# Strassen's identity for a feed-forward matrix of the first layer, token-major, with 16 transposes

## The chip, the cores and the metric

The kernel runs on one core of a Trainium2 chip. The metric is the device time of one execution in microseconds (us), the median of several runs. The core's engines work side by side and wait for each other through semaphores: PE (TensorE) multiplies matrices, DVE (VectorE) and ACT (ScalarE) do elementwise work, POOL (GpSimd) does a little of it, and SP, POOL and ACT issue DMA transfers. Results of PE land in PSUM, which has eight banks of 128 x 512 numbers here; all else lies in SBUF.

## The reference

A trunk of two layers over 256 tokens with 1024 features. Each layer is a token mixer (a gated linear recurrence in the first, causal attention with a bias by relative position in the second) followed by a feed-forward part, each with an RMS norm in front and a residual add behind; a last norm closes it.

```python
def swiglu(h, w13, w2):
    g, u = jnp.split(h @ w13, 2, axis=-1)
    return ((jax.nn.silu(g) * u) @ w2).astype(h.dtype)

for layer in range(2):
    h = h + mixer(rms_norm(h, norm_mix[layer]))
    h = h + swiglu(rms_norm(h, norm_ffn[layer]), ffn_w13[layer], ffn_w2[layer])
return rms_norm(h, final_norm)
```

w13 is 1024 x 5632 and w2 is 2816 x 1024, so the hidden width is 22 tiles of 128. Everything is float32.

## The kernel before

**Number format.** PE multiplies in a rounded format (`fp32r`). To keep float32's precision each operand is split into a high part (ACT, L448 for weights: `whi`) and the rest (DVE, L450: `wlo`), and each product is three matmuls: high x high, high x low, low x high. A product with a 128 x 128 weight as the stationary operand and 256 tokens as the moving one is `mm_w`; a product with 128 tokens of an activation as the stationary operand and 512 weight columns as the moving one, token-major, is `mm_x`.

**Weights.** All weights lie in DRAM in the order of their use (`weight_plan`), in units of 1024 columns. A unit is loaded by SP into one of the `raw` buffers (six, taken in turn), split into one of `NSUB` = 6 pairs `whi`, `wlo`, and then used. `make_subs` keeps the units coming some way ahead. `keep["from"]` holds the pairs back from reuse while a later part still reads them.

**Order of the work.** A planner (`Order`) writes out, while the program is built, the order of instructions on each engine. PE's main stream is fixed by the code; it advances the planner's clock `now` and a count of tiles. Every other operation has an estimated cost, what it depends on, and a due time in tiles; each engine's queue takes, among the operations that are ready, the one due first. An operation is ready 130 ns (`LAT`) after what it depends on. `od.need` makes the main stream wait in the plan. On the chip each engine then runs its list in that order and waits where semaphores tell it.

**First layer's feed-forward (`swiglu(0, ...)`).** For each hidden tile j: gate and up (48 matmuls, PSUM group A), then on ACT and DVE Sigmoid and three products, the split into `hh`, `hl`, and, four tiles later, the row j of w2 times this tile (`down0`, 24 matmuls, four banks of group B, feature-major: eight feature tiles of 128 x 256 tokens). The last two rows are taken bank by bank, and each finished bank goes to `residual`, which scales it by the norm's `row`, adds it to the residual `hT`, and makes the next layer's split input `x2`.

**Second layer's feed-forward.** Here w2 is taken by Strassen's identity already. Two hidden tiles make one step: a 2 x 2 block of tokens (two halves of 128) by hidden tiles, times a 2 x 2 block of hidden tiles by output columns (two halves of 512). Seven products m1 to m7 stand for eight. `combine` makes the sums of activations, `quad_sums` those of weights: one difference (`wdiff`), one sum on DVE (L480), one sum by an accumulating DMA on POOL's queue (L488; for the last step on DVE, L484). `early` takes m1, m2, m5 and `late` takes m4, m3, m6, m7; each m accumulates in a PSUM bank of its own over nine steps. The last four hidden tiles are not in steps: their rows go straight, by `mm_x`, into the banks of m6, m3, m7 and m2, which turns these into the four output quadrants. `fold` adds the other shares (m1, m5, m4, and m2 and m3 for a quadrant not their own) on DVE to `ht`, the residual turned to token-major by 16 transposes (L1334). The last step's folds, but that of m3, wait for the last weight split. `od.need` on `read` keeps PE from adding to m2 and m3 before their fold has read them.

Of the kernel before, what the change touches and what calls it, by code (L numbers as in the profile page):

```python
# [8 lines left out]
FT = mybir.dt.float32  # L9
# [6 lines left out]
P = 128  # L16
# [20 lines left out]
def quad(k):  # L37

    return [("ffn_w2", 1, k + a, 512 * b, 512) for a, b in ((0, 1), (1, 0), (1, 1), (0, 0))]


def weight_plan():
# [28 lines left out]
    def ffn(layer):  # L71
        for k in range(KT - 2):
            for j in range(4):
                plan.append(("ffn_w13", layer, k, P * j, P))
                plan.append(("ffn_w13", layer, k, DFF + P * j, P))
        for j in range(4):
            for half in range(2):
                column("ffn_w13", layer, half * DFF + P * j, (KT - 2, KT - 1))

        for j in range(4, FTN):  # L80
            column("ffn_w13", layer, P * j)
            column("ffn_w13", layer, DFF + P * j)
            if layer == 0:
                rows("ffn_w2", layer, j - 4)
            elif (j % 2 and 4 < j < FTN - 1) or j == FTN - 2:
                plan.extend(quad(j - 5 + j // (FTN - 2)))
        if layer == 0:
            for k in range(FTN - 4, FTN - 2):
                rows("ffn_w2", layer, k)
            last_rows("ffn_w2", layer, FTN)  # L90
        else:
            for k in range(FTN - 4, FTN):
                for nh in range(2):
                    plan.append(("ffn_w2", layer, k, 512 * nh, 512))
# [32 lines left out]
class Ring:  # L127
# [3 lines left out]
    def new(self, held=False):  # L131
        b = Buf(self)
        b.held = held
        return b

# [5 lines left out]
class Order:  # L141
# [38 lines left out]
    def free_at(self, ring):  # L180

        if len(ring.past) < ring.bufs:
            return 0.0
        b = ring.past[-ring.bufs]
# [24 lines left out]
    def emit(self, o, t):  # L209
# [11 lines left out]
        for b in o.alloc:  # L221
            b.tile = b.ring.make()
            b.ring.past.append(b)
# [87 lines left out]
def hybrid_trunk(ctx: ExitStack, tc: tile.TileContext, wts, xT, par, gfin, tab, onehot, masks, out):  # L311
# [29 lines left out]
    def lay_out():  # L341
# [13 lines left out]
        sb.tile([P, 16], FT, name="gape")  # L355
        for part in "hl":
            ring(f"e{part}0", [P, S], 1, FR).make()
        sb.tile([P, 48], FT, name="gapf")

# [32 lines left out]
    lay_out()  # L392
    segs, c0 = [], 0
# [5 lines left out]
    for i, e in enumerate(plan):  # L399
        if plan[i:i + 4] == quad(e[2]):  # L400
            quads[[a for a, _ in segs].index(c)] = e[2]
# [27 lines left out]
    def make_subs(upto):  # L429

        while ws["made"] < min(upto, len(subs)):
# [25 lines left out]
            ws["V"] = ov  # L457
            ws["made"] += 1
# [7 lines left out]
    diffs, sums = {}, {}  # L466
# [613 lines left out]
    for k in range(KT):  # L1080
# [14 lines left out]
    od.op("A", ca(P), lambda: A.activation(heads(tbh.tile), many, AF.Copy), reads=[tb], alloc=[tbh], due=80)  # L1095
    od.op("V", cv(P), lambda: V.tensor_tensor(heads(tbl.tile), many, heads(tbh.tile.bitcast(FT)), op=OP.subtract),
          reads=[tb, tbh], alloc=[tbl], due=80)
    od.op("A", ca(NOH), lambda: A.activation(ohr.tile, oh.tile, AF.Copy), reads=[oh], alloc=[ohr], due=80)
    for eb, c0, n in zip(ebs, (0, 384), (384, NOH - 384)):
        def biases(eb=eb, c0=c0, n=n):  # L1100
            mm(eb[:, :n], tbh.tile, ohr[:, c0:c0 + n], start=True)
            mm(eb[:, :n], tbl.tile, ohr[:, c0:c0 + n], stop=True)
        od.op("T", 500, biases, reads=[tbh, tbl, ohr], alloc=[eb], due=80)
        al = dict(writes=[e]) if c0 else dict(alloc=[e])
        od.op("A", ca(n), lambda eb=eb, c0=c0, n=n: A.activation(e[:, c0:c0 + n], eb[:, :n], AF.Copy), reads=[eb],
              due=80, **al)
# [49 lines left out]
    def swiglu(layer, x, stats, gu, down):  # L1156

        hs = {}

        def hidden(j, b):  # L1160
            gs = new("sgq", [P, S], 3)
            sg = new("u", [P, S], 3)
            due = 6
            od.op("V", cv(S), lambda: V.tensor_tensor(gs.tile, b[:, :S], stats.row.tile, op=OP.mult),
                  reads=[b, stats.row], alloc=[gs], due=due)
            od.op("A", ca(S), lambda: A.activation(sg.tile, gs.tile, AF.Sigmoid), reads=[gs], alloc=[sg], due=due)
            od.op("V", cv(S), lambda: V.tensor_tensor(gs.tile, gs.tile, sg.tile, op=OP.mult), reads=[sg], writes=[gs], due=due)
            od.op("V", cv(S), lambda: V.tensor_tensor(sg.tile, b[:, S:], gs.tile, op=OP.mult), reads=[b, gs], writes=[sg],
                  due=due)
            x = X("e", 0, 1) if (layer, j) in ((0, 0), (0, 11)) else X("h", j % 7)  # L1170
            hi, lo = x.h, x.l
            od.op("A", ca(S), lambda: A.activation(hi.tile, sg.tile, AF.Copy), reads=[sg], alloc=[hi], due=due + 6)
            od.op("V", cv(S), lambda: V.tensor_tensor(lo.tile, sg.tile, hi.tile.bitcast(FT), op=OP.subtract),
                  reads=[sg, hi], alloc=[lo], due=due + 6)
            hs[j] = x

        first_four(layer, [main_bank(gu) for _ in range(4)], x, hidden)
        for j in range(4, FTN):
            b = main_bank(gu)
            gate_up(layer, j, b, x)  # L1180
            hidden(j, b)
            b.held = False
            od.written(stats.row)
            down(j - 4, hs)
        for k in range(KT):
            x[k].free()
        down(FTN - 4, hs, last=True)
# [3 lines left out]
    acc = {}  # L1191

    def down0(k, hs, last=False):
        if not acc:
            acc[0] = [main_bank("B") for _ in range(4)]
        for kk in range(k, FTN if last else k + 1):
            out_rows("ffn_w2", 0, kk, hs, acc[0], FTN, lambda i: residual(i, acc[0][i], x2, 1, st2, st1.row, 4 * i))

    od.written(sto.row)
    swiglu(0, x1, st1, "A", down0)  # L1200


    st2.finish("B", 40)
# [3 lines left out]
    vv.ring.past.append(vv)  # L1207

# [96 lines left out]

    def more_raws():

        old, turn = rings["raw"], [0]

        def make():  # L1310
            turn[0] += 1
            return bt.tile[:, 2 * D:3 * D] if turn[0] % (RAW + 1) == 1 else old.make()
        rings["raw"] = Ring(make, RAW + 1)
        rings["raw"].past = [Buf(None)] + old.past[-RAW:]
        inside("wsum", D, SUB, 1)
# [7 lines left out]
    more_raws()  # L1323
# [85 lines left out]
    alias("uu", "mov", [P, 512])  # L1409
    alias("gu", "sqacc", [P, 512])  # L1410
    alias("wdiff", "yt", [P, 512])
    inside("xdiff", 0, P, 2, e)
    QUADS = (FTN - 4) // 2
    hs, ops, pair = {}, {}, {}

    def hidden1(j, b, copied):
        s = new("sgq", [P, S], 3)
        due = 2
        if copied:
            g = new("gu", [P, 512], 2)  # L1420
            od.op("A", ca(512), lambda b=b: A.activation(g.tile, b[:, :], AF.Copy), reads=[b], alloc=[g], due=0)  # L1421
            b = g
        od.op("V", cv(S), lambda: V.tensor_tensor(s.tile, b[:, :S], st3.row.tile, op=OP.mult),  # L1423
              reads=[b, st3.row], alloc=[s], due=due)
        od.op("A", ca(S), lambda: A.activation(s.tile, s.tile, AF.Silu), reads=[s], writes=[s], due=due)
        up = (b, lambda: b[:, S:])
        if j < 2 * QUADS:
            if j % 2 == 0:
                pair[j // 2] = new("uu", [P, 512], 2)
            u = pair[j // 2]  # L1430
            c = slice(j % 2 * S, j % 2 * S + S)
            od.op("V", cv(S), lambda: V.tensor_tensor(u[:, c], up[1](), s.tile, op=OP.mult), reads=[up[0], s], due=due,
                  **(dict(writes=[u]) if j % 2 else dict(alloc=[u])))
            if j % 2:
                combine(j // 2, u)
            return
        u = new("u", [P, S], 3)
        od.op("V", cv(S), lambda: V.tensor_tensor(u.tile, up[1](), s.tile, op=OP.mult), reads=[up[0], s], alloc=[u],  # L1438
              due=due)
        hs[j] = X("h", (4 * QUADS + j - 2 * QUADS) % 7)  # L1440
        split(hs[j], u, lambda: u.tile, S, due + 4)

    def split(x, b, src, n, due):
        hi, lo = x.h, x.l
        r = (lambda t: t) if n != "z" else lambda t: t.rearrange("p (z t) -> p z t", z=2)
        n = S if n == "z" else n
        od.op("A", ca(n), lambda: A.activation(r(hi[:, :n]), src(), AF.Copy), reads=[b], alloc=[hi], due=due)
        od.op("V", cv(n), lambda: V.tensor_tensor(r(lo[:, :n]), src(), r(hi[:, :n].bitcast(FT)), op=OP.subtract),
              reads=[b, hi], alloc=[lo], due=due)

    def combine(p, u):

        a, b, d = new("sgq", [P, S], 3), new("u", [P, S], 3), new("xdiff", [P, P], 2)
        due = 6
        ops[p] = {t: X("h", (4 * p + n) % 7) for n, t in enumerate("dacb")}
        od.op("V", cv(P), lambda: V.tensor_tensor(d.tile, u[:, :P], u[:, 384:], op=OP.subtract), reads=[u], alloc=[d],
              due=due)
        split(ops[p]["d"], d, lambda: d.tile, P, due)
        od.op("V", cv(S), lambda: V.tensor_tensor(a.tile, u[:, :S], u[:, S:], op=OP.subtract), reads=[u], alloc=[a],
              due=due)  # L1460
        split(ops[p]["a"], a, lambda: a.tile, S, due)
# [150 lines left out]
```

## Time and profile before

| | |
|---|---|
| Median of 3 runs | 609.55 us (609.29 to 609.84) |
| Profiled execution, its own time | 608.73 us |
| Span from its first to its last instruction | 607.0 us |
| Granted PE clock, mean | 0.997 |
| Busy: PE, DVE, ACT, POOL | 598.1, 476.2, 387.7, 53.4 us |
| First layer's feed-forward, tiles in their steady order | about 175 to 316 us |
| Second layer's feed-forward | about 433 to 601 us |

In the profile's rows a number such as x48 counts instructions, the first two numbers are start and duration in us (in lists by time), `psA<-whi,hh` means that the instruction wrote a tile of PSUM group A from the tiles `whi` and `hh`, and what stands in square brackets is idle time before it and what ended it. A row of busy time by stretch gives its bounds, its length, and for PE, PE's weight loads, DVE, ACT and POOL busy us and instructions, then the granted clock, the DMA engines' busy share and GB/s. Matmul ends are modelled; their starts show PE's pace.

### The profile page before, as it was taken

What the parts mean: (1) busy time and instruction counts of PE and PEld (TensorE: products, weight loads), DVE (VectorE), ACT (ScalarE), POOL (GpSimd) and SP (SyncE); (2) the same over time, 40 slices, a digit from 0 to 9 for tenths busy, and PEclk for the clock granted to TensorE, in tenths of its full rate; (3) what the DMA queues carried; (4) which work ended last, traced back from release to release, by engine and by line L of the source; (5) the groups of instructions that cost most, each with busy time, mean ns of one, the idle gap of its engine ahead of it and who ended that gap; (6) DMA issues with size and microseconds to landing.
All of it is one profiled execution on the core that took longest, in us unless ns stands there. A gap on an engine that the chain in (4) does not pass through costs nothing.

```text
span 607.0 us, 12428 instructions
## 1 busy us (share of the span) xinstructions
PE 598.1 (99%) x4783; PEld 579.3 (95%) x4783; DVE 476.2 (78%) x869; ACT 387.7 (64%) x761; POOL 53.4 (9%) x101
## 2 busy tenths in 40 slices
PE   9999999999999999999999999999999999999995
PEld 7899999999999999999998899999999999999985
DVE  6899988869665766666669578876889798889896
ACT  6798998947634554444447566664777576666763
POOL 0043131100321000000000100000000000000003
PEclk9999999999999999999999999999999999999998
DMA  8956543554799766656563564446475677678721
GB/s 290 348 174 201 182 141 118 164 172 134 212 188 258 271 189 195 197 188 205 182 202 113 202 215 167 144 150 229 158 200 169 225 234 236 203 255 237 205 70 69
DMA packets 34406, 116.68 MB, mean 192 GB/s; under 512 B 4683, under 2 KB 6219, under 8 KB 34348
## 3 DMA queue, kind: packets, MB, share of 16 engines
q1 hardware_dynamic: 31484, 109.05, 54.0%
q0 software_dynamic: 1904, 6.10, 6.3%
q10 hardware_dynamic: 960, 0.76, 0.5%
q8 instruction: 37, 0.61, 0.4%
q14 instruction: 21, 0.17, 0.1%
HBM read 114.51 MB, written 1.38 MB: 191 GB/s over the span
## 4 chain that ended last, share of the span: by engine, by line
PE 93%; DVE 5%; issue 1%; POOL 1%; ACT 0%; DVEq 0%; POOLq 0%; ACTq 0%
PE psB L532 51%; PE psA L532 41%; DVE wlo L450 2%; DVE xl L656 0%; POOL ny L706 0%; PE psB L1276 0%; DVE yt L722 0%; DVE hT L724 0%; DVE sqacc L674 0%; PE psA L1334 0%; DVE ii L1486 0%; ACT whi L448 0%; DVE u L1438 0%; PE psA L711 0%; DVE sgq L1423 0%
## 5 line engine op out<-in xcount | busy, mean ns | idle before, releaser
L450 DVE TENSOR_TENSOR wlo<-raw,whi 128x1024 fp32r<-128x1024 f32 (+1 forms) x200 | 238.8, 1204 | 79.2 <-ACT whi L448 78.5
L448 ACT ACTIVATE whi<-raw 128x1024 fp32r<-128x1024 f32 (+1 forms) x199 | 205.5, 1045 | 118.5 <-PE psA L532 48.5
L532 PE MATMUL psB<-xh,whi 128*128 128x256 f32 x608 | 171.4, 285 | 0.0
L532 PE MATMUL psB<-xh,wlo 128*128 128x256 f32 x608 | 166.5, 277 | 0.0
L532 PE MATMUL psB<-xl,whi 128*128 128x256 f32 x608 | 162.0, 277 | 0.0
L532 PE MATMUL psA<-xh,whi 128*128 128x256 f32 x544 | 151.1, 281 | 0.0
L532 PE MATMUL psA<-xh,wlo 128*128 128x256 f32 x544 | 148.7, 277 | 0.0
L532 PE MATMUL psA<-xl,whi 128*128 128x256 f32 x544 | 143.6, 277 | 0.0
L532 PEld LDWEIGHTS psB<-xh,wlo 128*128 128x128 f32 x608 | 114.5, 188 | 0.7
L532 PEld LDWEIGHTS psB<-xh,whi 128*128 128x128 f32 x608 | 114.4, 188 | 0.7
L532 PEld LDWEIGHTS psB<-xl,whi 128*128 128x128 f32 x608 | 111.4, 188 | 0.0
L532 PEld LDWEIGHTS psA<-xh,whi 128*128 128x128 f32 x544 | 102.3, 188 | 0.2
L532 PEld LDWEIGHTS psA<-xh,wlo 128*128 128x128 f32 x544 | 102.3, 188 | 0.0
L532 PEld LDWEIGHTS psA<-xl,whi 128*128 128x128 f32 x544 | 99.2, 188 | 0.0
L532 PE MATMUL psB<-hl,whi 128*128 128x256 f32 x160 | 44.2, 276 | 0.0
L532 PE MATMUL psB<-hh,whi 128*128 128x256 f32 x160 | 44.2, 276 | 0.0
L532 PE MATMUL psB<-hh,wlo 128*128 128x256 f32 x160 | 44.2, 276 | 0.0
L706 POOL TENSOR_TENSOR ny<-nv,mhalf 128x2 f32<-128x2 f32 x5 | 5.6, 1111 | 304.0 <-DVE nv L703 281.6
L532 PEld LDWEIGHTS psB<-hh,whi 128*128 128x128 f32 x160 | 30.0, 188 | 0.0
L532 PEld LDWEIGHTS psB<-hh,wlo 128*128 128x128 f32 x160 | 30.0, 188 | 0.0
L532 PEld LDWEIGHTS psB<-hl,whi 128*128 128x128 f32 x160 | 30.0, 188 | 0.0
L1421 ACT ACTIVATE gu<-psB 128x512 f32<-128x512 f32 x18 | 10.8, 598 | 26.3 <-PE psB L532 26.3
(239 smaller groups left out, 936.8 us busy)
## 6 DMA issues: line engine op xcount, KB each, us to landing
raw<-in_w_dram SPq DMA_DIRECT2D x193, 512.0 KB, 4.3
bt<-in_w_dram SPq DMA_DIRECT2D x9, 512.0 KB, 4.9
raw<-in_w_dram POOLq DMA_DIRECT2D x7, 512.0 KB, 5.4
hT<-in_x_dram SPq DMA_DIRECT2D x8, 128.0 KB, 5.0
raw<-in_w_dram SPq DMA_DIRECT2D x4, 256.0 KB, 4.6
bt<-scr POOLq DMA_DIRECT2D x16, 64.0 KB, 9.7
bt<-scr POOLq DMA_DIRECT2D x2, 256.0 KB, 11.6
bt<-in_final_dram ACTq DMA_DIRECT2D x1, 512.0 KB, 5.2
```

Of the source, the lines that this page charges most:

```text
L448: oa = od.op("A", ca(n), lambda h=h, r=src, o=o, n=n: A.activation(h[:, :n], r[:, o:o + n], AF.Copy), reads=[src], alloc=[h], due=due)
L450: ov = od.op("V", cv(n), lambda h=h, lo=lo, r=src, o=o, n=n: V.tensor_tensor(lo[:, :n], r[:, o:o + n], h[:, :n].bitcast(FT), op=OP.subtrac ...
L532: T.matmul(o, a, b, start=start, stop=stop, skip_group_check=True)
L706: od.op("G", 500, lambda: G.tensor_tensor(y.tile, v.tile, mhalf, op=OP.pow), reads=[v], alloc=[y], due=due)
L1421: od.op("A", ca(512), lambda b=b: A.activation(g.tile, b[:, :], AF.Copy), reads=[b], alloc=[g], due=0)
```

## The change

The second layer's code becomes a class `Strassen` that both layers use. In the first layer:

- All rows of w2 but the last four go in nine Strassen steps, with `gu` copies, Silu, `combine`, `quad_sums` and POOL's accumulating DMAs as in the second layer. Group A holds m1, m5, m4 and one bank for gate and up; group B holds m6, m3, m7, m2.
- The output quadrants are token-major, and there is no `ht` to add to: token half 0 goes to the first half of `vv` and half 1 to two `yq` buffers (in the place of `yt`). The first fold of each quadrant fills its buffer (a TENSOR_SCALAR), later ones add.
- The final four rows are taken in the order m6, m3, m7, m2. After each pair of quadrants, PE turns them by eight transposes into two banks of group B (`turned`), and `residual` adds these to `hT` with no further scaling.
- Raw buffers are handed out by the first that is free (`Slots`), with the second half of `vv` as a seventh during the first layer's steps, and two places in `bt` during the second layer's in the place of one.
- The position bias's operations get earlier due times, and its DMAs later and staggered ones.

```diff
+class Slots:
+    def first(self, order):
+        best = None
+        for s in self.slots:
+            t = None if not s[2] else 0.0 if s[1] is None else order.done(s[1])
+            if t is not None and (best is None or t < best[0]):
+                best = t, s
+        return best
...
+        def fold(self, i, *to):
+            m, col = self.m[i], self.stats.col
+            for tt, nh, plus, due in to:
+                c = col if plus else self.minus
+                q, at = self.quadrants[tt, nh]
+                first = (tt, nh) not in self.filled
+                self.filled.add((tt, nh))
+                def add(c=c, at=at, tt=tt, first=first):
+                    if first:
+                        V.tensor_scalar(at(), m[:, :], c[:, tt:tt + 1], None, op0=OP.mult)
+                    else:
+                        V.scalar_tensor_tensor(at(), m[:, :], c[:, tt:tt + 1], at(), op0=OP.mult, op1=OP.add)
+                kw = dict(alloc=[q]) if first and q.ring is not None else dict(writes=[q]) if first else {}
+                o = od.op("V", cv(512), add, reads=[m, c] if first else [m, q, c], due=due, **kw)
+                if i != 3:
+                    o.deps.append(self.behind)
...
+            if p == QUADS - 1:
+                self.behind = splits[w.i + 8]
+                self.fold(1, (0, 1, True, 35), (1, 0, True, 46))
+                self.fold(5, (0, 1, True, 35), (0, 0, False, 44))
+                self.fold(2, (1, 0, False, 45))
...
+                self.fold(4, (0, 1, True, 15), (1, 1, True, 25))
+                self.fold(3, (1, 0, True, 0))
...
+    f = Strassen(0, x1, st1, "A", {"A": (1, 5, 4), "B": (6, 3, 7, 2)}, quadrants)
+    w = {(k, nh): piece("ffn_w2", 0, k, 512 * nh, 512) for nh in range(2) for k in f.ks}
+    extra[2] = False
+    def turned(i, nh):
+        b = bank("B")
+        def turn():
+            for j in range(2):
+                for tt in range(2):
+                    c = 256 * (i % 2) + P * j
+                    T.transpose(b[:, S * j + P * tt:S * j + P * tt + P], quadrants[tt, nh][1]()[:, c:c + P], ident)
+        od.op("T", 450, turn, reads=[quadrants[tt, nh][0] for tt in range(2)], alloc=[b], due=0, early=700.0)
+        residual(i, b, x2, 1, st2, None, 2)
+    for nh, tt in ((0, 1), (0, 0), (1, 0), (1, 1)):
+        b = f.final[nh, tt]
+        f.wait_fold(nh, tt)
+        for k in f.ks:
+            mm_x(b[:, :], f.hs[k], w[k, nh], tt, stop=(k == FTN - 1))
+        wrote(b)
+        b.held = False
+        q, at = quadrants[tt, nh]
+        od.op("V", cv(512), lambda b=b, at=at, tt=tt: V.scalar_tensor_tensor(
+            at(), b[:, :], st1.col[:, tt:tt + 1], at(), op0=OP.mult, op1=OP.add), reads=[b, q, st1.col], writes=[q],
+            due=0).deps.extend(f.folds[tt, nh])
+        if (nh, tt) in ((0, 0), (1, 1)):
+            turned(2 * nh, nh)
+            turned(2 * nh + 1, nh)
...
-    od.op("G", 1000, lambda: G.dma_start(scr, e.tile), ...)           # bias operations ahead of this: due=80
+    od.op("G", 1000, lambda: G.dma_start(scr, e.tile), ...)           # bias operations ahead of this: due=40
-              nbytes=262144, due=90)
+              nbytes=262144, due=100 + r // 4)
-                  reads=[scr_b], writes=[bt], nbytes=65536, due=90)
+                  reads=[scr_b], writes=[bt], nbytes=65536, due=136 + r + 4 * j)
```

More of the change, by code (lines that the diff above doesn't have):

```diff
@@ L82, in ffn @@
             column("ffn_w13", layer, DFF + P * j)
[L83 to L94, printed above, removed]
+            if (j % 2 and 4 < j < FTN - 1) or j == FTN - 2:
+                plan.extend(quad(layer, j - 5 + j // (FTN - 2)))
+        last = [(k, nh) for k in range(FTN - 4, FTN) for nh in range(2)]
+        for k, nh in last if layer else sorted(last, key=lambda p: p[::-1]):
+            plan.append(("ffn_w2", layer, k, 512 * nh, 512))
     token_major("hgrn_w_in", 2 * D)
@@ L134, in new, with __init__, take @@
         return b
+class Slots:
+    def __init__(self, tiles):
+        self.slots = [[t, None, True] for t in tiles]
+    def new(self, held=False):
+        b = Buf(self)
+        b.held = held
+        return b
+    def first(self, order):
[5 more added lines that the diff above has]
+        return best
+    def take(self, b, order):
+        s = self.first(order)[1]
+        b.tile, s[1] = s[0], b
 class Op:
@@ L1154, in gate_up @@
         wrote(b)
[L1156 to L1162, printed above, removed]
-            due = 6
[L1164 to L1168, printed above, removed]
-                  due=due)
[L1170 to L1187, printed above, removed]
@@ L1207, in hybrid_trunk @@
     vv.ring.past.append(vv)
+    extra = [vv.tile[:, 1, :], None, True]
+    rings["raw"].slots.append(extra)
+    part0 = [Buf(None) for _ in range(2)]
+    quadrants = {(0, nh): (part0[nh], lambda nh=nh: vv[:, 0, 512 * nh:512 * nh + 512]) for nh in range(2)}
+    for nh in range(2):
+        yq = new("yq", [P, 512], 2)
+        quadrants[1, nh] = yq, lambda yq=yq: yq.tile
+    f = Strassen(0, x1, st1, "A", {"A": (1, 5, 4), "B": (6, 3, 7, 2)}, quadrants)
[24 more added lines that the diff above has]
+            turned(2 * nh + 1, nh)
+    for k in f.ks:
+        f.hs[k].free()
+    keep["from"] = None
+    free_subs(ws["sub"])
+    for i in (1, 4, 5):
+        f.m[i].held = False
+    od.need(lambda: 0.0 if extra[1] is None else od.done(extra[1]))
+    st2.finish("B", 40)
     vsplit = {}
@@ L1322, in hybrid_trunk @@
     st3.finish("A", 14)
-    more_raws()
+    for i in (1, 2):
+        rings["raw"].slots.append([bt.tile[:, D * i:D * i + D], None, True])
     gf = Buf(None)
@@ L1443, in split @@
[L1443 to L1461, printed above, removed]
-        split(ops[p]["c"], u, lambda: cut(u, 0, (384, 2), (1, P)), "z", due + 1)
-        od.op("V", cv(S), lambda: V.tensor_tensor(
-            b.tile.rearrange("p (z t) -> p z t", z=2), u[:, P:384].rearrange("p (z t) -> p z t", z=2),
-            cut(u, 0, (384, 2), (1, P)), op=OP.subtract), reads=[u], alloc=[b], due=due + 1)
-        split(ops[p]["b"], b, lambda: b.tile, S, due + 1)
@@ L1523, in hybrid_trunk @@
-    first_four(1, [main_bank("B") for _ in range(4)], x3, lambda j, b: hidden1(j, b, False))
-    for j in range(4, FTN):
-        if j < 7:
-            b = one = main_bank("B")
-        else:
-            last = b
-            od.need(lambda: None if any(o.end is None for o in last.readers) else max(o.end for o in last.readers))
-            b = Buf(None)
-            b.tile = one.tile
-        gate_up(1, j, b, x3)
-        b.held = j == 6
-        hidden1(j, b, True)
-        if j == 4:
-            od.op("A", ca(D), lambda: A.activation(gf.tile, gf.tile, AF.Copy, scale=2 * float(D) ** 0.5), reads=[bt],
-                  writes=[gf], due=30)
-        if j > 4:
-            (early if j % 2 and j < FTN - 1 else late)((j - 5) // 2)
-        if j == FTN - 2:
-            early(QUADS - 1)
```

277 lines of the change are left out of this document (157 added, 120 removed).

## The prediction

> **What bounds the kernel now.** I read the engine totals first, then the chain of work that ended last, in order of time, then the busy time of two stretches: the plain feed-forward of the first layer (168 to 307 us) and the Strassen feed-forward of the second (457 to 575 us).
>
> ```profile
> PE 598.1 (99%) x4783; PEld 579.3 (95%) x4783; DVE 476.2 (78%) x869; ACT 387.7 (64%) x761; POOL 53.4 (9%) x101
> ...
> PE 93%; DVE 5%; issue 1%; POOL 1%; ACT 0%; DVEq 0%; POOLq 0%; ACTq 0%
> ...
> 168.00:307.00 139.00, 139.00 (x1226) 139.00 (x1226) 89.11 (x122) 65.04 (x86) 5.26 (x10) 1.00 0.71 209
> 457.00:575.00 118.00, 118.00 (x881) 111.62 (x880) 104.41 (x156) 78.77 (x121) 6.12 (x7) 1.00 0.73 223
> ...
> 294.22 5.44 PE psA L532 x48
> 299.66 2.72 PE psB L532 x24
> ...
> 457.87 2.06 PE psA L532 x9
> 459.93 6.15 PE psB L532 x51
> 466.08 0.69 PE psA L532 x3
> 466.77 6.84 PE psB L532 x54
> 473.61 2.06 PE psA L532 x9
> ...
> 427.71 1.75 PE psA L1334 x16
> ```
>
> The reader is to see that PE is never idle in either stretch (139.00 of 139.00, 118.00 of 118.00). So PE work taken out is gained in full, and a PE wait put in is lost in full. The two layers differ in their cover: VectorE (third busy figure) has 89.11/139 = 64% in the first layer, 104.41/118 = 88% in the second. The chain rows give prices: a moving operand of 256 columns costs 5.44/48 = 0.113 us, one of 512 columns 2.06/9 = 0.229 us, a transpose 1.75/16 = 0.109 us. A hidden tile of the first layer costs 5.44 + 2.72 = 8.16 us (gate and up, then its row of w2); two of them, 16.32 us. In the second layer two hidden tiles with one Strassen step run from 457.87 to 473.61, 15.74 us.
>
> **The change part by part.** *The nine Strassen steps.* Each replaces 48 matmuls of 256 columns by 21 of 512: 5.44 - 21 x 0.229 = 0.63 us by count. By whole periods it is 16.32 - 15.74 = 0.58 us. I take the periods, since they hold the changes between banks too: 9 x 0.58 = 5.2 us off PE (5.7 by count).
>
> *The last four rows of w2*, token-major: 48 x 0.229 = 11.0 us in place of 4 x 2.72 = 10.9: +0.1.
>
> *The 16 transposes* go through PE between matmuls, +1.75 us. With nothing else, PE work falls by 5.2 - 0.1 - 1.75 = 3.35 us.
>
> *VectorE and ScalarE in the steady part.* The first layer takes over the second's load: four weight splits and two sums per step, the gate copies to SBUF, Silu for Sigmoid and two products. In the second layer that fits under PE without one idle moment, so I cost it at nothing; without that cover a split is late by its length. VectorE's eighth of time to spare is thin. Silu may ask ScalarE for one table load more, which lies in its free third.
>
> *Queues.* SP's loads become 7 for 6 in two hidden tiles, POOL gets eight accumulating DMAs, and the 18 DMAs of the position bias now share POOL's queue with them. The bias operations come earlier. Raw buffers by the first that is free change nothing while PE never waits for a load. These cost nothing as long as weight units stand ready; that cover is priced as a rival.
>
> *The end of the layer* is where I see a new wait. I take it from the end of the second layer, with the last product group there from 585.69, after which the final products begin at 588.43.
>
> ```profile
> 585.69 0.39 PE L532 MATMUL psB<-whi,hh 128*128 128x512 f32 x1
> 588.43 0.28 PE L532 MATMUL psB<-whi,hh 128*128 128x256 f32 x1
> ...
> 586.38 1.06 ACT L448 ACTIVATE whi<-raw 128x1024 fp32r<-128x1024 f32 x1
> ...
> 586.99 0.42 DVE L1423 TENSOR_TENSOR sgq<-gu,rrow 128x256 f32<-128x256 f32 x1
> 587.32 0.74 DVE L1486 SCALAR_TENSOR_TENSOR ii<-psA,ny,ii 128x512 f32<-128x512 f32 x1
> 587.98 1.22 DVE L450 TENSOR_TENSOR wlo<-raw,whi 128x1024 fp32r<-128x1024 f32 x1
> 589.12 0.42 DVE L1438 TENSOR_TENSOR u<-gu,sgq 128x256 f32<-128x256 f32 x1
> 589.45 0.74 DVE L1486 SCALAR_TENSOR_TENSOR ii<-psA,ny,ii 128x512 f32<-128x512 f32 x1
> 590.12 0.41 DVE L1448 TENSOR_TENSOR hl<-u,hh 128x256 fp32r<-128x256 f32 x1
> 590.45 0.74 DVE L1486 SCALAR_TENSOR_TENSOR ii<-psA,ny,ii 128x512 f32<-128x512 f32 x1
> 591.23 0.75 DVE L1486 SCALAR_TENSOR_TENSOR ii<-psB,ny,ii 128x512 f32<-128x512 f32 x1
> 591.89 0.74 DVE L1486 SCALAR_TENSOR_TENSOR ii<-psA,fm,ii 128x512 f32<-128x512 f32 x1
> ...
> 594.92 0.74 DVE L1486 SCALAR_TENSOR_TENSOR ii<-psA,ny,ii 128x512 f32<-128x512 f32 x1
> ...
> L1404 DVE TENSOR_SCALAR raw<-raw,fz x2: 380/384/389, 602.7 to 603.0; 128x320 f32<-128x320 f32 x2
> ```
>
> PE may not add the last four rows into bank m3 before the fold of m3 has read it. In the second layer that fold (587.32) waits for nothing else, since it adds into `ht`, which is filled already. In the first layer its target is a `yq` buffer that a fold of m1 must first fill, and this one must wait for the layer's last weight split (`behind`), with a due time of 46, after five other folds with 35, 44 and 45. The second layer's rows show that order: the m1 fold to this place is the last, at 594.92, over 5 us behind the first. So I rebuild VectorE's queue with these durations. The last split starts when its high part is made, 586.38 + 1.06 = 587.44, and takes 1.14 to the next start: 588.6. Then u of the last hidden tile (0.33): 588.95. Then six folds and one split of u, 6 x 0.66 + 0.34 = 4.3: 593.25. Four of the folds are fill operations of another form; by the TENSOR_SCALAR row, 0.384 us for 320 columns, 512 would be about 0.6, which takes 0.2 to 0.3 off. The planner calls an operation ready 130 ns after what it depends on, so behind the m1 fold the next weight unit (the value projection's first, 1.14) can slip in before m3's fold (0.74). m3 is read at 594.0 without and 595.1 with it. PE, after 12 products for m6, stands ready at 588.43 + 12 x 0.229 = 591.2. It waits 2.8 to 3.9 us; I take 3.4, the slip with cheap fills. The bounds are 0, if the folds come early enough, and 4.5, if VectorE is half a split later than here. Nothing else is queued for PE there: the transposes need the same quadrants.
>
> *After it.* Five of the six pairs of split weights are held until the final products end. The value projection's second unit is split after that, 1.06 + 1.22 = 2.3 us, under 12 products of its first unit (2.75 us) and eight transposes (0.9 us): nothing, or up to 1 us if VectorE has a residual in front. The residual loses its four scaling products. The first four feature tiles are turned two final quadrants before they are needed.
>
> ```profile
> 336.01 0.43 PE L711 MATMUL psB<-ident,ny 128*128 128x128 f32 x2 [0.62 <-POOL ny L706]
> ```
>
> PE waits here for POOL's power (0.62 us). I leave it in; it could go, 0.6 less.
>
> **The sum** against the profiled execution's span: 607.0 - 5.2 + 0.1 + 1.75 + 3.4 = 607.05. That execution took 608.73 and the median of the runs is 609.55, so 2.5 us lie around the span: 609.6.
>
> **The rivals.** *Faster: the folds are in time.* If m3's fold is done by 591.2 on that clock, the whole 3.35 us stay: 606.2. It decides at 2.8 to 3.9 us of VectorE time, the folds that would have to go elsewhere. For it: of the six only the one fold of m1 to that quadrant must be ahead of m3's. Against: the due times.
>
> *Slower: weight units late while the bias DMAs run.*
>
> ```profile
> 164.00:172.00 8.00, 8.00 (x72) 8.00 (x71) 7.40 (x15) 4.70 (x9) 3.21 (x7) 1.00 0.91 118
> 180.00:188.00 8.00, 8.00 (x73) 8.00 (x72) 3.40 (x6) 2.44 (x3) 3.08 (x6) 1.00 1.03 243
> 196.00:204.00 8.00, 8.00 (x73) 8.00 (x72) 7.19 (x11) 4.75 (x7) 0.00 (x0) 1.00 0.91 323
> ...
> ACT whi L448 <- DMA raw<-in_w_dram: 12.5, 7, 3.5
> ...
> 193.79 1.23 DVE L450 TENSOR_TENSOR wlo<-raw,whi 128x1024 fp32r<-128x1024 f32 x1 [1.31 <-ACT whi L448]
> 201.53 0.28 PE L532 MATMUL psB<-hh,wlo 128*128 128x256 f32 x1
> ...
> 457.32 1.22 DVE L450 TENSOR_TENSOR wlo<-raw,whi 128x1024 fp32r<-128x1024 f32 x1
> 465.46 0.39 PE L532 MATMUL psB<-wlo,hh 128*128 128x512 f32 x1
> ...
> 482.15 1.22 DVE L450 TENSOR_TENSOR wlo<-bt,whi 128x1024 fp32r<-128x1024 f32 x1
> 486.58 0.28 PE L532 MATMUL psB<-xh,wlo 128*128 128x256 f32 x1
> ```
>
> The DMA engines are full from 164 to 204 us (0.91 to 1.03 of their time), and ScalarE waits 12.5 us for raw weights between 156 and 200. PE feels nothing, since the split that ends at 195.0 is first used at 201.5: 6.5 us in hand. In the second layer a split that ends at 483.4 is used at 486.6: 3.2 us in hand. The first Strassen steps fall into the full stretch and ask for a sixth more loads. If the 12.5 us of lateness meet 3 us in hand, PE loses about 2 us there (0 to 4): 611.6 with the wait above. Against it: the bias DMAs start earlier, and the second layer's first step has 6.9 us in hand (a split ends at 458.5, its use is at 465.5).
>
> *Slower: the new gap halves PE's clock.*
>
> ```profile
> 600.50:603.70 3.20, 0.04 (x1) 0.00 (x0) 2.42 (x9) 1.65 (x6) 0.84 (x1) 1.00 0.36 145
> 603.80:607.00 3.20, 0.00 (x0) 0.00 (x0) 0.00 (x0) 0.00 (x0) 0.00 (x0) 0.50 0.47 164
> ```
>
> The granted clock goes from 1.00 to 0.50 some 3.2 us after PE's last work (600.54). A wait of 3.2 us or more could meet that; if PE then ran at half clock for as long again, it would lose 1.6 us: 611.2. [...]
>
> **How the numbers follow.** Wait of 2.8 to 3.9 us and nothing more, 40%: 609.6, between 608.4 and 610.7. Folds in time, or half so, 30%: 606.2 to 608.4. Late weights, 22%: 610.7 to 613. Half clock, 8%. Range 606.0 to 612.6, which leaves out the ends of both. A difference of 0.2% (1.2 us) is about what a measurement here can tell. Faster 0.32 (folds in time, and a little of the main case with the POOL wait gone), same 0.38, slower 0.30.
>
> **What would show it.** Right: 16.32 us of the first layer become 15.7 in the chain, with no PE gap in the steps after the first; near the layer's end PE idles once, about 3 us, and its releaser is a VectorE fold; that fold stands behind six others and perhaps a weight split. Wrong: no gap there (then 606), gaps near 190 to 210 us with ScalarE waiting for raw weights, or a granted clock of 0.5 behind the gap.

## The result, and the profile after

The changed kernel takes 614.59 us (median of 4 runs, 613.18 to 616.04) against 609.58 us for the kernel before on the same chip: a ratio of 1.0082, interval 1.0059 to 1.0106. It is slower by 5.0 us, where 609.6 was forecast and the range ended at 612.6. Its profiled execution took 616.04 us, with a span of 614.3 us and a mean granted clock of 0.992.

The engine totals, and the chain of work that ended last by engine, of the changed kernel:

```profile
PE 599.2 (98%) x4508; PEld 568.4 (93%) x4508; DVE 514.7 (84%) x938; ACT 414.3 (67%) x816; POOL 61.7 (10%) x109
...
PE 91%; DVE 4%; DMA 2%; issue 1%; ACT 1%; POOL 1%; DVEq 0%; POOLq 0%; ACTq 0%
```

PE runs 275 matmuls fewer, and is still busy as long as before (599.2 us for 598.1). DMA and ACT, which had next to nothing of the chain, now have 3% of it.

**The steps themselves came out as forecast.** The chain in order of time (start, length, what):

```profile
218.29 2.06 PE psB L556 x9
220.34 6.15 PE psA L556 x51
226.50 0.69 PE psB L556 x3
227.19 6.84 PE psA L556 x54
234.03 2.06 PE psB L556 x9
```

Two hidden tiles take 234.03 - 218.29 = 15.74 us, with no idle time in between.

**Early wait.** The same view, in the second and third step:

```profile
184.03 1.15 DVE wsum L504
...
185.46 11.54 DMA raw<-in_w_dram
...
197.09 1.06 ACT whi L471
...
198.83 1.22 DVE wlo L473
...
201.80 1.15 DVE wlo L473
```

and PE's own rows, with its idle time in brackets:

```profile
200.11 0.50 PE L556 MATMUL psA<-wlo,hh 128*128 128x512 f32 x1 [1.27 <-DVE wlo L473]
...
202.99 0.51 PE L556 MATMUL psB<-wlo,hh 128*128 128x512 f32 x1 [1.22 <-DVE wlo L473]
```

VectorE must have read the plain weights for its own sum (`wsum`) before POOL may add to them by its accumulating DMA; that DMA is issued at 185.46 and has landed 11.54 us later; its split comes too late, and PE waits twice. These two start 1.66 and 1.61 us after the matmul before them, where the pace is 0.229: 2.8 us lost. Four of the dozen matmuls behind the first also start late, by 0.1 us each, against the same ones in e5 below, which has no such wait. The early wait costs 3.2 us in all.

**Wait at the layer's end.** VectorE's queue, and PE's first final product into m3 (start, length, line, operation):

```profile
308.19 1.23 DVE L473 TENSOR_TENSOR wlo<-ii,whi 128x1024 fp32r<-128x1024 f32 x1 [0.53 <-ACT whi L471]
309.33 0.42 DVE L1253 TENSOR_TENSOR u<-gu,sgq 128x256 f32<-128x256 f32 x1
309.67 0.75 DVE L1311 TENSOR_SCALAR ii<-psA,ny 128x512 f32<-128x512 f32 x1
310.33 0.74 DVE L1311 TENSOR_SCALAR ii<-psA,fm 128x512 f32<-128x512 f32 x1
310.99 0.41 DVE L1263 TENSOR_TENSOR hl<-u,hh 128x256 fp32r<-128x256 f32 x1
311.32 1.53 DVE L1313 SCALAR_TENSOR_TENSOR ii<-psA,ny,ii 128x512 f32<-128x512 f32 x2
312.77 1.40 DVE L1311 TENSOR_SCALAR yq<-psA,ny 128x512 f32<-128x512 f32 x2
314.08 1.22 DVE L473 TENSOR_TENSOR wlo<-raw,whi 128x1024 fp32r<-128x1024 f32 x1
315.21 0.75 DVE L1313 SCALAR_TENSOR_TENSOR yq<-psB,ny,yq 128x512 f32<-128x512 f32 x1
```

```profile
316.01 0.79 PE L556 MATMUL psB<-whi,hh 128*128 128x512 f32 x1 [3.94 <-DVE yq L1313]
```

This is the predicted queue: last split, six folds, the next weight unit slipped in at 314.08, then m3's fold. PE's matmul before it started at 311.67, so the two starts are 4.34 us apart, 4.1 more than the pace.

**Half clock.** Busy time by stretch (bounds, length; PE, PE's weight loads, DVE, ACT, POOL; then the granted clock):

```profile
311.60:314.70 3.10, 0.47 (x3) 0.04 (x1) 3.06 (x5) 0.00 (x0) 0.00 (x0) 1.00 0.02 7
314.70:316.00 1.30, 0.00 (x0) 0.00 (x0) 1.26 (x3) 0.00 (x0) 0.00 (x0) 0.50 0.00 0
316.00:321.50 5.50, 5.49 (x13) 4.33 (x14) 1.50 (x2) 0.00 (x0) 0.00 (x0) 0.50 0.31 95
321.50:324.60 3.10, 3.10 (x20) 2.62 (x19) 1.46 (x3) 0.00 (x0) 0.00 (x0) 1.00 0.03 5
```

The clock falls to 0.50 while PE waits, and stays there for 5.5 us of work: eleven matmuls start 0.427 us apart in place of 0.229, and with the ones at either end PE loses 2.6 us.

**The balance.** I compare one stretch, from the same matmul of the first layer's token mixer to the same matmul of the second layer's: two rows of before, then two of the changed kernel.

```profile
131.38 0.28 PE L532 MATMUL psB<-xh,wlo 128*128 128x256 f32 x1
...
358.32 0.28 PE L532 MATMUL psA<-xh,whi 128*128 128x256 f32 x1
```

```profile
132.63 0.28 PE L556 MATMUL psB<-xh,wlo 128*128 128x256 f32 x1
...
344.47 0.43 PE L735 MATMUL psB<-ident,ny 128*128 128x128 f32 x2 [0.73 <-POOL ny L730]
...
365.86 0.28 PE L556 MATMUL psA<-xh,whi 128*128 128x256 f32 x1
```

It grew from 226.94 to 233.23 us, by 6.3: +3.2 early wait, +4.1 wait at the end, +2.6 half clock, +0.1 POOL's power (0.73 for 0.62 us of idle time). That leaves -3.7 for PE's work, where the forecast had -3.35. The spans differ by 7.3; the other 1.0 is the start, which came 1.25 us later, less 0.2 behind the stretch. The change does not touch the start: over the profiles of this case but e9's, that first matmul starts between 130.8 and 132.6 us. From 24 to 48 us PE's matmuls of 256 columns start 0.118 us apart here and 0.113 to 0.114 in the kernel before; e10, an edit of the kernel before, has 0.118 as well, and no row shows why. Below, "the stretch" is the one between the two matmuls, and its length is free of that chance. This profile is the slowest of the four executions, 1.45 us above their median.

### The profile page after: what moved, and what is told of

Its sections match the earlier page's. It is cut to its first block, busy times and chain, and to the rows that moved or that the text cites. A ratio compares the mean times of both kernels' runs of the same rounds, so it can differ in the third digit from the quotient of the medians.

```text
span 614.3 us, 12015 instructions
## 1 busy us (share of the span) xinstructions
PE 599.2 (98%) x4508; PEld 568.4 (93%) x4508; DVE 514.7 (84%) x938; ACT 414.3 (67%) x816; POOL 61.7 (10%) x109
## 4 chain that ended last, share of the span: by engine, by line
PE 91%; DVE 4%; DMA 2%; issue 1%; ACT 1%; POOL 1%; DVEq 0%; POOLq 0%; ACTq 0%
PE psB L556 48%; PE psA L556 41%; DMA raw<-in_w_dram 2%; DVE wlo L473 2%; DVE ii L1313 1%; POOL ny L730 0%; PE psB L1471 0%; ACT whi L471 0%; PE psA L1519 0%; DVE hl L1263 0%; DVE xl L680 0%; DVE yq L1311 0%; PE psB L1375 0%; DVE sqacc L698 0%; DVE hT L750 0%
## 5 line engine op out<-in xcount | busy, mean ns | idle before, releaser
L473 DVE TENSOR_TENSOR wlo<-raw,whi 128x1024 fp32r<-128x1024 f32 (+1 forms) x186 | 220.5, 1203 | 26.8 <-ACT whi L471 26.2
L471 ACT ACTIVATE whi<-raw 128x1024 fp32r<-128x1024 f32 (+1 forms) x185 | 188.2, 1037 | 51.3 <-PE psA L556 25.1
L556 PE MATMUL psB<-whi,hh 128*128 128x512 f32 (+1 forms) x91 | 35.8, 394 | 4.1 <-DVE yq L1313 3.9
L556 PE MATMUL psB<-wlo,hh 128*128 128x512 f32 (+1 forms) x91 | 35.9, 395 | 1.2 <-DVE wlo L473 1.2
L556 PE MATMUL psB<-whi,hl 128*128 128x512 f32 (+1 forms) x91 | 36.0, 396 | 0.0
L1241 ACT ACTIVATE sgq<-sgq 128x256 f32<-128x256 f32 x44 | 18.2, 415 | 25.5 <-DVE sgq L1239 25.4
L556 PE MATMUL psA<-wlo,hh 128*128 128x512 f32 (+1 forms) x75 | 28.6, 381 | 1.3 <-DVE wlo L473 1.3
L512 POOL DMA_DIRECT2D raw<-in_w_dram x13 | 11.3, 872 | 178.3 <-DVE wsum L504 162.7
L556 PE MATMUL psA<-whi,hl 128*128 128x512 f32 (+1 forms) x75 | 28.6, 381 | 0.0
L556 PE MATMUL psA<-whi,hh 128*128 128x512 f32 (+1 forms) x75 | 28.3, 377 | 0.0
```

The source lines that it names most:

```text
L471: oa = od.op("A", ca(n), lambda h=h, r=src, o=o, n=n: A.activation(h[:, :n], r[:, o:o + n], AF.Copy), reads=[src], alloc=[h], due=due)
L473: ov = od.op("V", cv(n), lambda h=h, lo=lo, r=src, o=o, n=n: V.tensor_tensor(lo[:, :n], r[:, o:o + n], h[:, :n].bitcast(FT), op=OP.subtrac ...
L512: od.op("G", 1000, lambda: nc.gpsimd.dma_start(b.tile, wts[c0 // CHUNK], accum_op=OP.add), writes=[b], nbytes=2 * 524288, due=due + 1)
L556: T.matmul(o, a, b, start=start, stop=stop, skip_group_check=True)
```

## The experiments

Ten are edits of the changed kernel, two (e10, e14) of the kernel before. Ratios are to the kernel before, run on the same chip beside them; the stretch is that of the profiled execution.

| kernel | median us | ratio, interval | the stretch, us |
|---|---|---|---|
| before / changed | 609.58 / 614.59 | 1.0082 (1.0059 to 1.0106) | 226.9 / 233.2 |
| e1 m1's fold first | 609.80 | 1.0013 (1.0002 to 1.0024) | 227.1 |
| e2 PE kept busy | 612.72 | 1.0060 (1.0042 to 1.0079) | 230.9 |
| e3 bias DMAs late | 619.51 | 1.0168 (1.0154 to 1.0181) | 239.0 |
| e5 fold first, bias spread | 606.53 | 0.9955 (0.9943 to 0.9967) | 224.6 |
| e6 bias spread alone | 610.51 | 1.0019 (1.0008 to 1.0030) | 229.0 |
| e7 fold first, bias by ScalarE | 625.87 | 1.0274 (1.0260 to 1.0287) | 243.6 |
| e8 fold first, sums on DVE | 606.46 | 0.9955 (0.9943 to 0.9967) | 224.6 |
| e9 e5, all powers dearer | 612.00 | 1.0038 (1.0024 to 1.0052) | 226.1 |
| e10 before, one power dearer | 608.62 | 0.9984 (0.9975 to 0.9992) | 226.5 |
| e11 e8, one power dearer | 604.13 | 0.9913 (0.9899 to 0.9926) | 222.8 |
| e13 due 44.5 | 613.59 | 1.0062 (1.0049 to 1.0075) | 232.3 |
| e14 before, bias times alone | 609.13 | 0.9995 (0.9986 to 1.0004) | 226.8 |

**e1: is it the order of the folds?**

```diff
-self.fold(1, (0, 1, True, 35), (1, 0, True, 46))
+self.fold(1, (0, 1, True, 35), (1, 0, True, 46 if self.layer else 34))
```

> The changed kernel, with m1's fold to quadrant (1, 0) due first among the first layer's folds (34 in place of 46); the second layer is as it was. Theory, the order of the folds: m3's fold is then behind one or two folds instead of six and a weight split, so the 4.1 us that PE idles at 312 to 316 us go, and with them the half clock of 2.6 us behind it (13 matmuls at 0.427 in place of 0.229 us): 614.6 - 6.7 = 607.9. Rival, VectorE as a whole is too late at the layer's end: the wait moves to a later quadrant, a gap of 2 us or more stays in the profile, and the time is above 611.

609.80 us. PE's idle time at the layer's end shrinks to 0.28 us, and the granted clock is back at 0.997. So one due time made both the wait and the half clock. The early wait stays (2.1 us in this execution), and PE waits longer for POOL at the norm:

```profile
310.80 0.50 PE L556 MATMUL psB<-whi,hl 128*128 128x512 f32 x1 [0.28 <-DVE hl L1263]
...
338.87 0.43 PE L735 MATMUL psB<-ident,ny 128*128 128x128 f32 x2 [1.53 <-POOL ny L730]
```

That wait is 0.8 us more than in the changed kernel, and the wait of 0.28 us costs 0.6 us with the slower matmul behind it; both are part of what is missing to the 607.9 expected. PE did not come to the norm earlier: in the changed kernel it began to wait 2.08 us after POOL's power had started, here 2.41 us. The power itself took longer, 3.89 us for 2.76. POOL's row in the changed kernel, then in e11 below, which has the fold first too:

```profile
341.66 2.76 POOL L730 TENSOR_TENSOR ny<-nv,mhalf 128x2 f32<-128x2 f32 x1 [56.45 <-DVE nv L727]
...
332.00 3.89 POOL L734 TENSOR_TENSOR ny<-nv,mhalf 128x2 f32<-128x2 f32 x1 [51.04 <-DVE nv L731]
```

**e2: is the half clock a matter of PE's idleness?** Sixteen matmuls of the identity into a free bank stand in the gap; the trace has them as 32 instructions, 0.111 us apart. (`f.one`, the free bank, is set in a line that is not shown.)

```diff
+if (nh, tt) == (0, 0):
+    for _ in range(16):
+        mm(f.one[:, :P], ident, ident, start=True, stop=True)
 f.wait_fold(nh, tt)
...
```

> The changed kernel, with 16 matmuls of the identity into a free PSUM bank ahead of m3's final products, about 3.4 us of PE work inside the 4.1 us wait; they add nothing to the result. Theory, the idle PE loses its clock: the wait stays as long as it is, the granted clock stays at 1.0 behind it, and 2.6 us go: 612.0. Rival, the clock falls for another reason or the slow matmuls are slow by the chain of waits: nothing gained, 614.6 or more.

612.72 us: m3's fold comes as late as before (PE's first final product into m3 starts at 314.58, 4.35 us after its last one for m6), but the clock stays at 1.00 behind it:

```profile
315.00:316.00 1.00, 1.00 (x6) 0.83 (x5) 0.90 (x2) 0.00 (x0) 0.00 (x0) 1.00 1.01 352
```

The mean clock is 0.997 to 0.999 in all six executions, where the changed kernel's four have 0.992 or 0.993. The time falls by 1.9 us between the medians, and by 1.4 against the kernel before beside each; the two intervals overlap, so the clock is the firmer sign.

**e13: what is the weight split that slipped in worth, and how long a gap halves the clock?**

```diff
 self.fold(1, (0, 1, True, 35), ...
-(1, 0, True, 46))
+(1, 0, True, 46 if self.layer else 44.5))
```

> The changed kernel, where m1's fold to the quadrant of m3 gets a due time of 44.5 in place of 46: it moves one fold ahead (in front of m4's to the last quadrant), so that this fold, and not a weight split, stands between it and m3's fold. PE's order is the same. The gap of 4.34 us becomes 4.34 - 1.13 = 3.2. Theory A (the weight split that slips in costs 1.1 us, and PE's clock is halved only after an idle time longer than that): 614.6 - 1.1 - 2.6 = 610.9. Theory B (the clock is halved after 3.2 us as well): 614.6 - 1.1 = 613.5 or a little less.

613.59 us, and theory B by the clock. m3's fold runs right behind the six folds (VectorE, then PE):

```profile
313.32 1.40 DVE L1311 TENSOR_SCALAR yq<-psA,ny 128x512 f32<-128x512 f32 x2
314.64 0.74 DVE L1313 SCALAR_TENSOR_TENSOR yq<-psB,ny,yq 128x512 f32<-128x512 f32 x1
```

```profile
315.44 0.51 PE L556 MATMUL psB<-whi,hh 128*128 128x512 f32 x1 [2.80 <-DVE yq L1313]
```

The gap between the starts is 3.18 us, 1.16 less. Yet the clock is halved again, 0.8 us after PE has taken up its work (busy time by stretch):

```profile
312.30:315.40 3.10, 0.34 (x2) 0.00 (x0) 3.05 (x5) 0.00 (x0) 0.00 (x0) 1.00 0.00 0
315.40:316.24 0.84, 0.81 (x3) 0.67 (x4) 0.82 (x2) 0.00 (x0) 0.00 (x0) 1.00 0.00 0
316.24:319.66 3.42, 3.42 (x10) 2.63 (x9) 1.72 (x2) 0.00 (x0) 0.00 (x0) 0.50 0.37 115
```

That the time, too, is theory B's is luck in this execution. The halved stretch is only half as long as in the changed kernel, and PE does not wait for ny; but from 200 us to the layer's end PE's matmuls of 256 columns start 0.118 us apart, where they start 0.113 apart before 200 us and in the other profiles. That costs about 2.7 us, and no row shows why.

**e6: is the early wait the bias DMAs, apart from the folds?** They are held back by the loads of later steps, three at a time.

```diff
+steps = sorted(si for si in quads if si < len(segs) // 2)
+turn = iter(range(18))
...                          # the same for the DMAs due at 100
-due=136 + r + 4 * j)
+due=136 + r + 4 * j).deps.append(Issued(steps[1 + next(turn) // 3] + 2))
```

> The changed kernel with the bias DMAs alone spread: three behind the loads of each of steps 2 to 7, instead of up to eight together ahead of the first accumulating DMA. Theory (the early wait, 2.8 us over PE's pace, comes of the bias DMAs standing with the first steps' weights; the wait at the layer's end and the halved clock behind it are another matter): the early gaps go, the later ones stay: 614.6 - 2.8 = 611.8. Rival (the gain of the spread was there only because the folds had moved too, or the first steps' loads are late by themselves): an early gap of 1.5 us or more stays, 613 to 614.6.

610.51 us. No early gap is left; the gap at the layer's end is 4.34 us as before. It is 4.1 us faster where 2.8 was expected. In the profiles the stretch is 4.2 us shorter: 3.2 for the whole early wait, and 0.9 because PE, in the same order as in the changed kernel, does not wait for ny. POOL's power took 1.62 us here and not 2.76. The executions also differ: in six of the eleven the mean clock is 0.995 or 0.996 (609.1 to 610.5 us) and not 0.992 or 0.993 (610.6 to 612.1), so the halved stretch is not equally long in every execution.

**e5: both edits together.**

> The changed kernel, with m1's fold to (1, 0) first, and the bias DMAs three at a time behind the accumulating DMAs of six steps. Theory, both waits and the half clock go: 614.6 - 6.7 - 2.8 = 605.1, against 606.2 by the prediction's sum without any wait (3.35 us of PE work less). Rival, the PE work that Strassen saves is eaten elsewhere in the first layer: 608 or more with no PE gap over 0.5 us before 340 us in the profile.

606.53 us, faster than before. The stretch is 224.6 us. It holds 0.6 for the short wait at the layer's end and 0.9 for POOL's longer one (1.53 for 0.62 us), so PE's work fell from 226.9 by 3.8 us, and not by the 3.35 of the forecast. What the bias DMAs do to the loads is seen in the DMA issues from 176.0 to 185.4 us (KB each, us to landing), first in the changed kernel, then in e5, then in e8:

```profile
raw<-in_w_dram SPq DMA_DIRECT2D x1, 512.0 KB, 14.2
...
raw<-in_w_dram SPq DMA_DIRECT2D x1, 512.0 KB, 3.2
...
raw<-in_w_dram SPq DMA_DIRECT2D x1, 512.0 KB, 10.7
```

**e8: the sum of the first two steps on VectorE.**

```diff
+if si in sorted(quads)[:2]:
+    od.op("V", cv(SUB), lambda: V.tensor_tensor(b.tile, a.tile, b.tile, op=OP.add), reads=[a], writes=[b],
+          due=due + 1).deps.append(loads[si + 1])
+    return
 od.op("G", 1000, lambda: nc.gpsimd.dma_start(b.tile, wts[c0 // CHUNK], accum_op=OP.add), ...)
```

> With m1's fold first, the second weight sum of the first two steps is taken by VectorE (two additions of 1024 columns, about 1.15 us each) in place of the accumulating DMA; the bias DMAs stay where the change put them. Theory A (the accumulating DMA is what is late): the early gaps go, 608.1, as VectorE waits idle there. Theory B (the plain weight loads are late as well, the DMA engines being full): ScalarE still waits for raw weights and PE with it, a gap of 0.5 to 1.5 us stays, 608.6 to 609.8.

606.46 us, and no early gap. The loads are still late (10.7 us above), as theory B has it; but PE can bear that, as theory A has it. The wait needs both: a full set of DMA engines (0.93 to 1.05 of their time from 156 to 188 us in the changed kernel), and a second transfer chained behind the first, load, then `wsum`, then the accumulating DMA. (e8 takes two of these transfers off the DMA engines as well, and its loads are somewhat faster for it or by chance.) Plain loads on SP's queue suffer as POOL's do (14.2 us in the changed kernel and 3.2 in e5, beside the 11.54 us of POOL's accumulating DMA), and the accumulating DMA was issued 0.3 us after `wsum` had ended (185.17, 185.46), so a place behind other DMAs in POOL's queue is not what kept it from starting.

**e7: the bias DMAs issued by ScalarE.** `A.dma_start` in place of `G.dma_start` for the 18 of them.

> With m1's fold first, the 18 bias DMAs are issued by ScalarE in place of POOL, at the same due times. Theory A (a place in POOL's queue: the accumulating DMA is late because it was issued behind eight bias DMAs on one queue): the early gaps, 1.7 us over pace with m1's fold first, go: 609.8 - 1.7 = 608.1. Theory B (the DMA engines are full, whoever issues): the accumulating DMA lands as late, the gaps stay, 609.8 or a little more for ScalarE's issuing.

625.87 us: it does not tell the two theories apart, since it makes a worse wait first. ScalarE stands in its own queue until earlier bias DMAs have landed, and every weight split and gate copy with it (chain of waits, then PE):

```profile
158.23 13.79 DMA bt<-scr
...
172.04 4.22 DMA bt<-scr
```

```profile
180.50 0.58 PE L556 MATMUL psA<-xh,whi 128*128 128x256 f32 x1 [16.80 <-DVE uu L1247]
```

**e3: the bias DMAs after the last accumulating DMA.** `.deps.append(Issued(step9 + 4))`, where step9 is the last step's load.

> The changed kernel, with the 18 DMAs of the position bias issued after the last of the first layer's accumulating DMAs (near 295 us instead of 158 to 184). Theory, they make the second step's accumulating DMA and the raw loads late: the two PE waits at 200 and 203 us (2.8 us together) go, 614.6 - 2.8 = 611.8, and the wait at 312 stays. Rival, the Strassen steps load too much for the DMA engines by themselves: a wait of over 1 us stays between 185 and 215 us. Second rival: the bias DMAs now hold up the units of the layer's end or POOL's power for the norm, and the time comes back there.

619.51 us. The early gaps are gone, but the same DMAs now meet the loads for the layer's end. A load issued at 294.00 lands 17.15 us later (chain); PE waits 6.68 us, and 3.76 us more for m3's fold, with the half clock behind both:

```profile
294.00 17.15 DMA ii<-in_w_dram
```

```profile
314.58 0.80 PE L556 MATMUL psB<-whi,hh 128*128 128x512 f32 x1 [6.68 <-ACT hh L1263]
...
320.15 0.80 PE L556 MATMUL psB<-whi,hh 128*128 128x512 f32 x1 [3.76 <-DVE yq L1314]
```

So at this late place, too, these transfers are not free when they come all at once.

**e14: the bias times in the kernel before.** Due times 40, 100 and 136 as in the change.

> The kernel before with the change's due times of the bias alone: its operations earlier (40 in place of 80), its DMAs at 100 to 136 and later in place of 90. Theory (the bias DMAs cost only where a second set of transfers, the accumulating ones, is chained behind the loads): no change, 609.4, within 609.0 to 609.9. Rival (the new times are bad by themselves): PE gaps between 160 and 205 us, 610.5 or more.

609.13 us, no difference, and no early gap, though the DMA engines are as full as in the changed kernel (0.93 to 1.06 of their time from 156 to 188 us, 0.93 to 1.05 there). The new times alone do no harm; they do it where accumulating DMAs follow the loads.

**e10, e9, e11: POOL's power.** The planner takes it to last 0.5 us.

```diff
-od.op("G", 500, lambda: G.tensor_tensor(y.tile, v.tile, mhalf, op=OP.pow), ...)
+od.op("G", power, lambda: G.tensor_tensor(y.tile, v.tile, mhalf, op=OP.pow), ...)   # 2800
```

> m1's fold first and the bias DMAs spread (606.5), and the planner told that POOL's power takes 2.8 us in place of 0.5. Theory (PE waits 1.7 us over its pace before the transposes of ny because its order puts them where a power of 0.5 us would be done): other products come ahead of them, the wait goes: 606.5 - 1.6 = 604.9. Rival (PE has nothing else to do there, or what waits for the transposed row is then late): 606.2 to 607.

> The kernel before with the same edit to the planner's cost of POOL's power, in the same norm. PE's order changes in one place only: 13 products go ahead of the transposes of ny. Theory: the gap of 1.01 us (0.78 over pace) goes, 609.4 - 0.8 = 608.6. Rival (a wait later takes its place): 609.4.

> m1's fold first, the first two steps' second weight sum on VectorE (606.46 so far), and the planner told that POOL's power takes 2.8 us in place of 0.5 in the norm behind the first feed-forward layer alone. Theory (PE's 1.93 us between two starts there, 1.7 over its pace, is a matter of where the transposes of ny stand in its order; 13 products more ahead of them cover it): 606.5 - 1.7 = 604.8. Rival (the values' copies need the same ny, so that PE then waits a little later for free banks): 606 to 606.7.

e9 set 2800 for every norm: 612.00 us. The wait for ny behind the first feed-forward layer goes, but the order around the earlier norms, where the power takes 0.7 to 1.1 us in the changed kernel, gets worse: PE waits at 39.5, 40.8, 117.0 and 145.0 us, 4.9 us in all, and the last of these halves the clock. e10 and e11 set it for the one norm. In e10 12 matmuls and in e11 10 move ahead of the transposes (13 were expected), and the wait goes: the kernel before gains 0.9 us, and e11 takes 604.13 us, the best version here, 0.87% below before. Busy time by stretch of e11:

```profile
156.00:204.00 48.00, 48.00 (x382) 46.28 (x382) 44.42 (x76) 32.51 (x53) 10.82 (x19) 1.00 0.88 211
204.00:300.00 96.00, 96.00 (x709) 90.47 (x708) 86.49 (x126) 65.05 (x98) 4.33 (x5) 1.00 0.76 232
300.00:318.00 18.00, 17.72 (x92) 14.75 (x91) 16.07 (x25) 6.22 (x12) 0.00 (x0) 1.00 0.46 160
318.00:345.00 27.00, 27.00 (x145) 23.02 (x143) 21.94 (x33) 20.01 (x32) 3.89 (x1) 1.00 0.60 211
```

PE is idle 0.28 us in 189, with VectorE at 93% and 90% in the first two stretches. The stretch of 222.8 us is 226.94 - 0.78 for POOL's gap of before, + 0.6 for the short wait at the layer's end, - 3.9 for PE's work.

## Why the prediction was wrong, step by step

- *PE's work.* The forecast -3.35 us was right in its parts and about 0.4 us too small: what is left after the waits is -3.7 in the changed kernel, -3.8 in e5 and e8 and -3.9 in e11. The price by count, which I set aside (5.7 in place of 5.2), would have given -3.85. Which of the parts holds the 0.4 is not shown.
- *VectorE and ScalarE at nothing in the steady part:* right; 15.74 us with no idle time, and in e8 with two sums more on VectorE. The table load more that Silu was allowed is there too: six of 1.28 us on ScalarE, where the kernel before has five, the new one at 160.14 us, with PE busy all the time from 156 to 164.
- *The wait at the end.* The mechanism was right in each part (order of six folds, the split that slips in, m3's fold), and shown by e1. The size was 4.1 where I took 3.4. The forecast's own terms gave 3.6 to 3.7 with the slip and cheap fills (3.9 less 0.2 to 0.3), so 3.4 was low by a slip of arithmetic. The fill operations are no cheaper than the others (0.74 and 0.75 us, 0.66 from start to start; I had gone by a row of 320 columns out of SBUF), which gives 3.9 back, and the other 0.2 are mostly pauses between operations that depend on each other (the two at 311.32 take 1.45 us to the next start, where 1.32 would be their pace). The bound of 4.5 held it.
- *Queues at nothing, late weights as a rival at 22%.* The rival came true, at 3.2 us where I had "about 2 (0 to 4)". What I had missed is the chain: I argued from the 6.5 us in hand for a split behind one load, but the accumulating DMA is a second load behind the first, and in the full stretch each takes over 10 us (15.0, the median of SP's five raw loads issued from 160 to 176 us, and 11.54).
- *Half clock as a rival at 8%.* It came true too, at 2.6 us where I had 1.6. I had let the half clock last as long as the wait; it lasted 6.8 us, 5.5 of them work. My condition, a wait of 3.2 us or more, was met by the very value I took for the main case, so its 8% contradicted the 40% given to "3.4 us and nothing more".
- *The step that failed* is therefore "How the numbers follow", with the sum that it rests on: late weights and the half clock stand at nothing in the sum and come in only as rivals, each added to the wait alone (611.6 and 611.2), never to each other, while one lies 110 us ahead of the wait and the other follows from it. By the forecast's own prices the three together are 609.6 + 2 + 1.6 = 613.2, which is already past the range's end of 612.6. The sum with all as measured is 607.05 - 0.4 + 0.7 + 3.2 + 2.6 + 0.1 = 613.25 for the span, and 614.3 with the start 1.25 us later and the 0.2 behind it.
- *Folds in time, 606.2:* not what happened, but e8 shows the number. With the folds in time and the early wait gone it is 606.46 us. By the stretch, e8 is 1.0 us above that forecast (224.6 for 223.6): it still holds the 0.6 and 0.9 us of waits named under e5, less what PE's work fell beyond 3.35.
- *POOL's power left in:* right for the change (0.73 for 0.62 us). That the power's length is not fixed (3.89 us in e1 with a wait of 1.53, 1.62 in e6 with none), and that an order in the plan removes the wait, I did not say.

Not settled is why the early wait was 2.1 us in e1's profile and 3.2 in the changed kernel's, with the same code there.

## What to carry to other kernels

Ask of each rival whether it excludes the others: waits at different places, and a clock that follows from a wait, add up, and the range must hold their sum. Where a transfer is chained behind a transfer, slack must be counted twice over when the DMA engines are full (here 15.0 us for a load and 11.54 for the accumulating DMA behind one). Before a change is given up, look at the due time of the one operation that frees what PE needs next: here one number was worth 4.8 us between the medians, and 4.4 against the kernel before beside each.

## What the runs showed of the hardware

The halved clock came in stretches of 3.4 us: one in e13 (316.24 to 319.66), two in the changed kernel (314.69 to 321.52), four in e3 (from about 311.5 to 325.1). It also came with less idleness than I thought: in e9 PE was idle 1.74 us, and the clock fell 0.6 us after its return, for 3.4 us (busy time by stretch):

```profile
143.20:144.90 1.70, 0.07 (x1) 0.00 (x0) 1.70 (x4) 0.45 (x2) 0.00 (x0) 1.00 0.72 219
144.90:145.60 0.70, 0.59 (x5) 0.59 (x6) 0.70 (x3) 0.70 (x3) 0.00 (x0) 0.99 0.54 217
145.60:149.00 3.40, 3.40 (x19) 3.40 (x18) 3.40 (x8) 3.40 (x8) 0.00 (x0) 0.50 0.02 5
```

An idle time of 1.53 us (e1, e5, e8) halved nothing. Of the 3.41 us ahead of the fall PE worked 23% in the changed kernel, 24% in e13 and 49% in e9. The changed kernel's early wait left it 1.86 of the 3.41 us from 198.64 us on, 55%, and the clock stayed at 1.00.

The fall did not come at one distance from PE's last work before the wait: 2.6 us behind it in the changed kernel, and 3.6 in e13 and 2.3 in e9, where PE was at work again. The changed kernel's last fall, at 611.65 us, lies 290.13 us behind the return at 321.52, which is 42.5 times the 6.83 us of the halved clock before it, or 85 times half of that. These times suggest that the stretch that counts does not start with the wait; no run here moves a wait to test it. With the clock halved, 3.41 us of which PE worked 60% (e6, from 310.10) or 61% (the changed kernel, from 314.69) were followed by as much again at half clock; those next ones were fully busy, and the full clock came behind them. So one wait cost one halved stretch in e13 and two in e6's profile and the changed kernel, which would fit the two groups of e6's executions; what decides between one and two is not shown.

POOL's power on 128 x 2 numbers had no one length. At the norm behind the first feed-forward it took 2.75 us in the kernel before, 2.76 in the changed kernel, 3.89 or 3.90 in e1, e5, e7, e8, e9 and e11, and 1.62 in e6 and e13; in the changed kernel's other norms it took 0.69 to 1.07. At this norm it starts while a weight split runs on VectorE with others right behind it, two in a row in the changed kernel and three in e1, and its lengths are 1.13 us apart, a split's time from start to start. That the splits hold it up fits these rows; no edit was made to show it. And issuing 64 KB DMAs from ScalarE was not free: 15 of them held its queue for 16.8 us in e7.
